# A hybrid decoder layer: 24 of 26 pairs of input-projection blocks in the seven-product form, the convolution one channel group at a time beside the heads, its norm late

## The chip, the core and the metric

The kernel runs on one core of a Trainium2 chip. Five engines work side by side, each through its own queue of instructions, in an order fixed when the program is built: TensorE (PE in the profile; its weight loads are PEld), VectorE (DVE), ScalarE (ACT), GpSimd (POOL) and SyncE (SP, which here only issues DMAs). They wait for each other through semaphores. The metric is device time in microseconds; a time without "median" is that of one profiled execution.

## The reference, cut to what matters

512 tokens of 2048 features are normalised and projected to 6664 features: three groups of 512 for a convolution branch, eight heads' queries, keys, values and gates (1024 each) with one forget logit per head, and queries and gates of a cross-attention (512 each). The three branches give 2048 features, projected back to 2048 and added to x; a final RMSNorm follows.

```python
h = rmsnorm(x, norm_g[l])
proj = h @ w_in[l]
u = cv_a * jax.nn.sigmoid(cv_b)
u = causal_depthwise_conv(u, conv_w[l], conv_b[l])          # 31 taps, per channel
u = jax.nn.silu(layernorm(u, conv_ln_g[l], conv_ln_b[l]))   # over the 512 channels
y_conv = (u @ w_conv_pw[l]) * jax.nn.silu(cv_gate)
logf = jax.nn.log_sigmoid(f_logit + b_f[l])                 # c = cumsum over the tokens
y_fox = fox_attention(fq, fk, fv, logf) * jax.nn.silu(fox_gate)
y_mem = memory_attention(mq, mk, mv) * jax.nn.silu(mem_gate)
x = x + jnp.concatenate([y_conv, y_fox, y_mem], -1) @ w_out[l]
```

Everything is float32. The kernel splits each operand of a large product into a high part (a cast to a shorter float32 form, by ScalarE) and a low part (the difference, by VectorE) and adds three matmuls: high x high, high x low, low x high.

## The kernel before

**Blocks.** Work goes by blocks of 128 output features. A weight block of 2048 x 128 arrives in two halves of [128, 8, 128] (`raw`, six buffers) and becomes `whi` and `wlo` (three buffers each). The normalised x, transposed, lies in sixteen 128-feature tiles as `hh` (high) and `hl` (low). `project` makes a plain block: 16 feature tiles x 3 matmuls (`mm3`, L104 to L106) over all 512 tokens.

**The seven-product form.** `pair` makes two blocks together. It cuts features and tokens into halves and forms seven products in place of eight, each of 8 feature tiles x 3 matmuls over 256 tokens (L729). For that it needs sums of quarters of h: `first_sums` makes s1, s2, s3 (tiles `s0`, `s1`, `s2` in the trace, each with a high part h and a low part l) through the temporary tiles `t`; `last_sum` makes a fourth, `s4`, and writes it over the quarter of h that holds features 0 to 1023 of tokens 256 to 511, after the last plain projection has read it. Per pair, VectorE makes seven `wlo`, four differences of weight blocks (`less`, L699) and two sums for the second block's output `col` (L696).

**The stages.** (1) Memory keys and values, x's norm (scaled on ScalarE, L212), its transposes. (2) Convolution inputs `C_A`, `C_B` for four channel groups, all plain, with the forget logits (`forget_logits`, `log_sigmoid`, `forget_columns`) between the first and the fourth. (3) Four memory queries and gates, plain, with their attention. (4) Four convolution gates, plain, with `first_sums` beside them, then the pointwise projection. (5) Eight heads: a pair for query and key, a pair for gate and value; the first of the sixteen pairs is plain (`PLAIN = 1`), and `last_sum` follows it. (6) The output projection, in steps.

**The convolution.** Each group's 31 taps are operations of 128x512 on one accumulator, the first on ScalarE (L323), thirty on VectorE (L328). They go to a list, `bg`, and `background(n)` takes n of them behind each projection of stages 2 and 3. Four accumulators stay in SBUF. `centre` and `normalise` make the norm over channels in the middle of stage 3's last head: a sum over the four groups, a matmul with `mean_r` for the mean over partitions, the same for the squares, Ln and Exp on ScalarE for the root, three VectorE steps, a multiplication of each group, then Silu and the split into `csh`/`csl`.

**The order.** Program order is not the order on the engines: a scheduler at build time orders each engine's instructions as they become ready in its own timeline. The pieces of order below are what it made of each version.

Of the kernel before, what the change touches and what calls it, by code (L numbers as in the profile page):

```python
# [10 lines left out]
F32 = mybir.dt.float32  # L11
# [6 lines left out]
P = 128  # L18
S = 512
# [15 lines left out]
PLAIN = 1  # L35
# [12 lines left out]
def hybrid_layer_kernel(  # L48
# [100 lines left out]
    cd = dr.tile([NH, S], F32, name="cd")  # L149

# [10 lines left out]
    mkv = mpool.enter_context(tc.tile_pool(name="mkv", bufs=1, side="right"))  # L161
# [5 lines left out]
    with tc.tile_pool(name="start", bufs=1) as st:  # L167
# [129 lines left out]
    def project(f0, per=0):  # L297
# [5 lines left out]
        background(per)  # L303
        return o

    def silu_of(pool, o, tag, bufs):

        sg = pool.tile([P, S], F32, tag=tag, name=nm(tag), bufs=bufs)
        nc.scalar.activation(sg, o, AF.Silu)
        return sg  # L310

# [3 lines left out]
    with tc.tile_pool(name="conv", bufs=1, reuse_waits="tile") as cp:  # L315
        cs = [tuple(cp.tile([P, S], F32R, name=f"cs{w}{c}") for w in "hl") for c in range(NC)]
        acc = [cp.tile([P, S], F32, tag=f"acc{c}", name=f"acc{c}") for c in range(NC)]

        def taps_of(c, up):
            a = acc[c]  # L320

            def first():
                nc.scalar.activation(  # L323
                    a, up[:, 0:S], AF.Identity, scale=cwt[:, c, 0:1], bias=conv_b_c(c)
                )

            def tap(j):
                return lambda: nc.vector.scalar_tensor_tensor(  # L328
                    a, up[:, j : j + S], cwt[:, c, j : j + 1], a, ALU.mult, ALU.add
                )  # L330

            bg.append(first)
            bg.extend(tap(j) for j in range(1, TAPS))

        def conv_in(c):
            oa = project(C_A + c * P, 6)
            ob = project(C_B + c * P, 6)
            up = cp.tile([P, PAD + S], F32, tag="up", name=nm("up"), bufs=3)
            nc.gpsimd.memset(up[:, 0:PAD], 0.0)
            sg = cp.tile([P, S], F32, tag="sgb", name=nm("sgb"), bufs=2)  # L340
            nc.scalar.activation(sg, ob, AF.Sigmoid)
            nc.vector.tensor_tensor(up[:, PAD:], oa, sg, ALU.mult)
            taps_of(c, up)

        def mem_query(ma, h):
            o = project(M_Q + h * P, 7)
            qh = ma.tile([P, S], F32R, tag="qh", name=nm("qh"), bufs=1)
            ql = ma.tile([P, S], F32R, tag="ql", name=nm("ql"), bufs=1)
            split(qh, ql, o)
            return qh, ql  # L350

        def mem_probs(ma, h, q):
            qh, ql = q
            pr = []
            for i2 in range(2):
                sp = at((P, 2, M))
                for j in range(2):
                    sl = slice((2 * i2 + j) * P, (2 * i2 + j + 1) * P)
                    mm3(sp[:, j, :], (qh[:, sl], ql[:, sl]), (mk[0][:, h, :], mk[1][:, h, :]), True, True)
                ng = ma.tile([P, 2], F32, tag="ng", name=nm("ng"), bufs=4)  # L360
                nc.vector.tensor_reduce(ng, sp, AX.X, ALU.max, negate=True)
                nc.vector.tensor_scalar(ng, ng, SC, None, ALU.mult)
                pp = ma.tile([P, 2, M], F32, tag="pp", name=nm("pp"), bufs=2)
                sm = ma.tile([P, 2], F32, tag="sm", name=nm("sm"), bufs=4)
                for j in range(2):
                    nc.scalar.activation(
                        pp[:, j, :], sp[:, j, :], AF.Exp,
                        bias=ng[:, j : j + 1], scale=SC, accum_out=sm[:, j : j + 1],
                    )
                nc.vector.reciprocal(sm, sm)  # L370
                for j in range(2):
                    nc.scalar.mul(pp[:, j, :], pp[:, j, :], sm[:, j : j + 1])
                pr.append(pp)
            return pr

        def mem_attend(ma, h, pr, gate):
            pts = []
            for mt in range(MT):
                tp = at()
                for i in range(NT):  # L380
                    nc.tensor.transpose(
                        tp[:, i * P : (i + 1) * P], pr[i // 2][:, i % 2, mt * P : (mt + 1) * P], ident
                    )
                th = ma.tile([P, S], F32R, tag="th", name=nm("th"), bufs=2)
                tl = ma.tile([P, S], F32R, tag="tl", name=nm("tl"), bufs=2)
                split(th, tl, tp)
                pts.append((th, tl))
            ov = at()
            for mt in range(MT):
                hs = slice(h * P, (h + 1) * P)  # L390
                mm3(ov, (mv[0][:, mt, hs], mv[1][:, mt, hs]), pts[mt], mt == 0, mt == MT - 1)
            nc.vector.tensor_tensor(gate, ov, gate, ALU.mult)
            nc.gpsimd.dma_start(out=yd[12 + h], in_=gate)

        fgs = {}

        def forget_logits(fg):
            wf = fg.tile([P, KT, NH], F32, name="wf")
# [3 lines left out]
            wfs = fg.tile([P, KT, P], F32R, name="wfs")  # L402
# [6 lines left out]
            f2 = fg.tile([2 * NH, S], F32, name="f2")  # L409
            nc.vector.tensor_copy(f2, fo[: 2 * NH, :])  # L410
            fl = fg.tile([NH, S], F32, name="fl")
            nc.gpsimd.dma_start(out=fl, in_=f2[NH : 2 * NH, :])
            fgs.update(f2=f2, fl=fl)

        def log_sigmoid(fg):
            z, e = fgs["f2"][:NH, :], fgs["fl"]
            nc.vector.tensor_tensor(z, z, e, ALU.add)
            nc.vector.tensor_scalar(z, z, bf_t, None, ALU.add)
            nc.vector.scalar_tensor_tensor(e, z, -1.0, z, ALU.mult, ALU.max)
            nc.scalar.activation(e, e, AF.Exp, scale=-1.0)  # L420
            u = fg.tile([NH, S], F32, name="u")
            nc.vector.tensor_scalar(u, e, 1.0, None, ALU.add)
            lu = fg.tile([NH, S], F32, name="lu")
            nc.scalar.activation(lu, u, AF.Ln)
            nc.vector.scalar_tensor_tensor(e, u, -1.0, e, ALU.add, ALU.subtract)
            nc.vector.reciprocal(u, u)
            nc.vector.tensor_tensor(e, e, u, ALU.mult)
            nc.vector.tensor_tensor(lu, lu, e, ALU.subtract)
            HALF = S // 2
            cs = [fg.tile([NH, HALF + S], F32, name=f"cs{i}") for i in range(2)]  # L430
            for t in cs:
                nc.vector.memset(t[:, :HALF], 0.0)
            nc.vector.scalar_tensor_tensor(cs[0][:, HALF:], z, 0.0, lu, ALU.min, ALU.subtract)
            cur, step = 0, 1

            def double(a, b, step):
                return lambda: nc.vector.tensor_tensor(
                    b[:, HALF:], a[:, HALF:], a[:, HALF - step : HALF - step + S], ALU.add
                )

            adds = []
            while step < S:
                adds.append(double(cs[cur], cs[1 - cur], step))
                cur, step = 1 - cur, 2 * step
            c = cs[cur][:, HALF:]
            adds.append(lambda: nc.gpsimd.dma_start(out=cd, in_=c))
            fgs["c"] = c
            for f in reversed(adds):
                bg.appendleft(f)

        def forget_columns():
            c = fgs["c"]
            pc = at((P, NT * NH))
            for i in range(NT):
                nc.tensor.transpose(
                    pc[:, i * NH : (i + 1) * NH], c[:, i * P : (i + 1) * P], ident[:NH, :NH]
                )
            nc.vector.tensor_scalar(ccol.rearrange("p i h -> p (i h)"), pc, -1.0, None, ALU.mult)
        conv_in(0)
        with tc.tile_pool(name="fg", bufs=1, reuse_waits="tile") as fg:  # L460
            forget_logits(fg)
            conv_in(1)
            log_sigmoid(fg)
            conv_in(2)
            forget_columns()
        conv_in(3)
        with tc.tile_pool(name="matt", bufs=1, reuse_waits="tile") as ma:

            gates = []
# [607 lines left out]
```

## Time and profile before

| what | value |
|---|---|
| median of 3 runs (lowest to highest) | 873.48 us (871.82 to 873.68) |
| the profiled execution | 872.15 us |
| its span, first to last instruction | 870.3 us |
| mean granted TensorE clock | 0.995 |
| TensorE matmuls | 5562 |
| taps on VectorE (L328) | 120, 747 ns the median |
| DMA | 107.52 MB, mean 124 GB/s |

A line of the timeline has start, duration, engine, line, operation, output and inputs with their shapes, and a count; an idle time before it stands in brackets. Durations of neighbours on one engine overlap a little, so the distance from one start to the next is what an operation costs in a full queue. A matmul's own duration (about 0.4 us for 512 columns) is longer than the distance to the next, since matmuls are pipelined. The activity by fortieths of the span (tenths busy):

```
PE   8999999999999999999999999999999999999996
DVE  4656699999956987877777777777777895876964
ACT  5894342225456643577565665657574852443523
```

Stage 2 and 3 are slices 4 to 12, the gates 13 to 15, the heads up to 31, the outputs the rest.

### The profile page before, as it was taken

How to read it: one execution, taken by the hardware profiler on the slowest of the kernel's cores; microseconds unless marked ns; L12 is line 12 of the kernel's file. 1: busy time of each engine (PE TensorE's matmuls, PEld its weight loads, DVE VectorE, ACT ScalarE, POOL GpSimd, SP SyncE). 2: the span in 40 equal slices, each digit the busy share in tenths (PEclk: the TensorE clock that was granted, in tenths of full speed). 3: DMA queues.
4: the chain of work that ended last, by engine and by line, in shares of the span. 5: the costliest groups of instructions: out<-in, count | busy, mean ns of one | idle time of the engine just before them, and what ended most of it. 6: DMA issues, size and time to landing. Idle time of an engine off the chain costs nothing.

```text
span 870.3 us, 13950 instructions
## 1 busy us (share of the span) xinstructions
PE 855.7 (98%) x5562; PEld 774.9 (89%) x5562; DVE 656.8 (75%) x948; ACT 463.8 (53%) x734; POOL 37.9 (4%) x76
## 2 busy tenths in 40 slices
PE   8999999999999999999999999999999999999996
PEld 6887887888888888999999999999999988998995
DVE  4656699999956987877777777777777895876964
ACT  5894342225456643577565665657574852443523
POOL 1001000000000002010001000000000000000001
PEclk9999999999999999999999999999999999999998
DMA  9972234333342334243434343333334745351415
GB/s 325 352 193 57 73 97 111 97 78 92 85 109 62 108 97 134 73 121 98 111 88 117 97 103 101 100 95 103 109 98 126 262 154 186 98 194 49 146 49 193
DMA packets 143265, 107.52 MB, mean 124 GB/s; under 512 B 3892, under 2 KB 126816, under 8 KB 142560
## 3 DMA queue, kind: packets, MB, share of 16 engines
q1 hardware_dynamic: 141696, 102.52, 40.4%
q0 software_dynamic: 1504, 4.11, 1.4%
q8 instruction: 43, 0.70, 0.3%
q14 instruction: 22, 0.18, 0.1%
HBM read 98.46 MB, written 8.14 MB: 122 GB/s over the span
## 4 chain that ended last, share of the span: by engine, by line
PE 96%; DVE 1%; issue 1%; DMA 1%; ACT 0%; SPq 0%; POOL 0%; POOLq 0%; ACTq 0%
PE pj L729 34%; PE pj L104 13%; PE pj L105 13%; PE pj L106 13%; PE pj L978 8%; PE at L104 3%; PE at L106 3%; PE at L105 3%; PE at L817 1%; DMA raw<-in_w_mem_kv_dram 1%; PE pj L262 0%; PE at L262 0%; PE pj L407 0%; PE pj L408 0%; PE at L778 0%
## 5 line engine op out<-in xcount | busy, mean ns | idle before, releaser
L93 ACT CAST whi<-raw 128x1024 fp32r<-128x1024 f32 x205 | 214.9, 1050 | 302.6 <-PE pj L105 115.1
L94 DVE TENSOR_TENSOR wlo<-raw,whi 128x1024 fp32r<-128x1024 f32 x205 | 250.2, 1222 | 121.2 <-ACT whi L93 116.7
L105 PE MATMUL pj<-hl,whi 128*128 128x512 f32 x352 | 139.6, 396 | 0.0
L106 PE MATMUL pj<-hh,wlo 128*128 128x512 f32 x352 | 139.4, 396 | 0.0
L104 PE MATMUL pj<-hh,whi 128*128 128x512 f32 x352 | 139.3, 396 | 0.0
L729 PE MATMUL pj<-hh,whi 128*128 128x256 f32 x480 | 135.4, 282 | 0.0
L729 PE MATMUL pj<-hl,whi 128*128 128x256 f32 x480 | 135.0, 281 | 0.0
L729 PE MATMUL pj<-hh,wlo 128*128 128x256 f32 x480 | 134.8, 281 | 0.0
L699 DVE TENSOR_TENSOR raw<-raw,raw 128x1024 f32<-128x1024 f32 x76 | 92.6, 1219 | 0.7
L729 PEld LDWEIGHTS pj<-hh,whi 128*128 128x128 f32 x480 | 90.5, 188 | 0.1
L729 PEld LDWEIGHTS pj<-hl,whi 128*128 128x128 f32 x480 | 90.5, 188 | 0.1
L729 PEld LDWEIGHTS pj<-hh,wlo 128*128 128x128 f32 x480 | 90.5, 188 | 0.0
L328 DVE SCALAR_TENSOR_TENSOR acc<-up,cwt,acc 128x512 f32<-128x512 f32 x120 | 84.5, 744 | 1.2 <-ACT acc L323 0.9
L978 PE MATMUL pj<-whi,rh 128*128 128x256 f32 x448 | 79.9, 279 | 0.7 <-DVE sst L1032 0.4
L104 PEld LDWEIGHTS pj<-hh,whi 128*128 128x128 f32 x352 | 66.1, 188 | 15.9 <-DVE hl L97 0.2
L106 PEld LDWEIGHTS pj<-hh,wlo 128*128 128x128 f32 x352 | 66.1, 188 | 15.7
L105 PEld LDWEIGHTS pj<-hl,whi 128*128 128x128 f32 x352 | 66.2, 188 | 15.5
L978 PEld LDWEIGHTS pj<-whi,rh 128*128 128x128 f32 x448 | 68.8, 188 | 1.3 <-DVE res L904 1.1
L978 PE MATMUL pj<-wlo,rh 128*128 128x256 f32 x224 | 62.3, 279 | 0.0
L978 PEld LDWEIGHTS pj<-wlo,rh 128*128 128x128 f32 x224 | 42.1, 188 | 0.2
L729 PE MATMUL pj<-s0l,whi 128*128 128x256 f32 x120 | 34.4, 286 | 0.0
L729 PE MATMUL pj<-s0h,whi 128*128 128x256 f32 x120 | 34.3, 286 | 0.0
(295 smaller groups left out, 1676.7 us busy)
## 6 DMA issues: line engine op xcount, KB each, us to landing
raw<-in_w_in_dram SPq DMA_DIRECT2D x104, 512.0 KB, 3.8
raw<-in_w_out_dram SPq DMA_DIRECT2D x32, 512.0 KB, 4.6
raw<-in_w_mem_kv_dram SPq DMA_DIRECT2D x12, 512.0 KB, 7.3
xr<-in_x_dram SPq DMA_DIRECT2D x4, 1024.0 KB, 7.9
res<-in_x_dram SPq DMA_DIRECT2D x8, 512.0 KB, 7.2
out_dram<-res SPq DMA_DIRECT2D x16, 256.0 KB, 2.7
rs<-yd SPq DMA_DIRECT2D x15, 256.0 KB, 4.9
mr<-in_mem_dram SPq DMA_DIRECT2D x8, 256.0 KB, 7.3
```

Of the source, the lines that this page charges most:

```text
L93: ins = nc.scalar.copy(hi, src)
L94: nc.vector.tensor_tensor(lo, src, hi.bitcast(F32), ALU.subtract)
L104: nc.tensor.matmul(o, ah, bh, start=start, stop=False)
L105: nc.tensor.matmul(o, ah, bl, start=False, stop=False)
L106: nc.tensor.matmul(o, al, bh, start=False, stop=stop)
L328: return lambda: nc.vector.scalar_tensor_tensor(a, up[:, j : j + S], cwt[:, c, j : j + 1], a, ALU.mult, ALU.add)
L699: nc.vector.tensor_tensor(o, p, q, ALU.subtract)
L729: nc.tensor.matmul(o, p[:, k, :], q, start=start and k == 0 and i == 0, stop=k == HK - 1 and i == 2, skip_group_check=True,)
L817: nc.tensor.transpose(tp[:, (i - j) * P : (i - j + 1) * P], pr[i][:, j * P : (j + 1) * P], ident)
L978: nc.tensor.matmul(o[:, m, :], p, q[:, k, :], start=start and k + m + i == 0, stop=k == HK - 1 and i == 2, skip_group_check=True,)
```

## The change

- `PLAIN` and `plain_pair` are gone. Plain are only group 0's convolution inputs and memory head 0's query and gate. Memory heads 1 to 3, all head pairs, convolution groups 1 to 3 and the four convolution gates (two pairs) use `pair`: 24 of 26.
- `first_sums` and `last_sum` run at once, around memory head 0's two projections, with doubled temporary tiles; the log-sigmoid and its running sum (nine doublings, `cs`) follow in the program.
- The convolution pairs stand behind heads 0, 2 and 4. Each group has one `up` and one `acc`; its taps go to `bg`, of which each of a pair's seven products takes one; then the accumulator is stored to DRAM (`accd`) through GpSimd's queue.
- Behind head 6, the head tiles are given up for a norm pool, the four accumulators are read back, and the two gate pairs follow. `centre` and `normalise` come behind the first gate pair (squares now on ScalarE), the pointwise projection behind the second, then the head tiles again for head 7.
- x's row scaling moves from ScalarE to VectorE; the memory keys and values move to the other side of SBUF.

```diff
-            nc.scalar.mul(xrows[t], xrows[t], rs)
+            nc.vector.tensor_scalar(xrows[t], xrows[t], rs, None, ALU.mult)
...
+    with tc.tile_pool(name="fg", bufs=1, reuse_waits="tile") as fg:
+        oa, ob = project(C_A), project(C_B)
+        conv_channels(0, [oa], ob)
+        forget_logits(fg)
+        with tc.tile_pool(name="stmp", bufs=2, reuse_waits="tile") as stmp:
...
+            for g in range(4):
+                first_sums(tmp, g)
+            oq, og = project(M_Q), project(M_G)
+            for g in range(4):
+                last_sum(tmp, g)
+        forget_columns(log_sigmoid(fg))
...
+            background(1)
...
+    def conv_channels(c, xs, gate):
+
+        background(len(bg))
+        up = cp.tile([P, PAD + S], F32, tag="up", name=nm("up"))
+        acc = cp.tile([P, S], F32, tag="acc", name=nm("acc"))
...
+        bg.append(first)
+        bg.extend(tap(j) for j in range(1, TAPS))
+        bg.append(lambda: nc.gpsimd.dma_start(out=accd[c], in_=acc))
...
+    def open_norm():
+        lp = ln["pool"] = lnpool.enter_context(tc.tile_pool(name="ln", bufs=1, reuse_waits="tile"))
+        background(len(bg))
+        acc = ln["acc"] = [lp.tile([P, S], F32, name=f"la{c}") for c in range(NC)]
+        for c in range(NC):
+            nc.gpsimd.dma_start(out=acc[c], in_=accd[c])
...
+    def after_gates(i):
+        def f(xs, col):
...
+            if i == 0:
+                centre()
+                normalise()
+            else:
+                project_conv()
+                lnpool.close()
+                open_fox()
...
+    work = [(M_Q + h * P, M_G + h * P, after_mem(h)) for h in range(1, NM)]
+    for h in range(NH):
+        work.append((F_Q + h * P, F_K + h * P, after_qk(h)))
+        work.append((F_G + h * P, F_V + h * P, after_gv(h)))
+        if h in (0, 2, 4):
+            c = h // 2 + 1
+            work.append((C_A + c * P, C_B + c * P, after_conv(c)))
+        if h == NH - 2:
+            for i in range(2):
+                g = C_G + 2 * i * P
+                work.append((g, g + P, after_gates(i)))
```

In the new kernel the split's low part is L93, `mm3` is L103 to L105, the seven products are L493, the weight differences L463, the taps L367.

**First place: VectorE behind the weights of memory head 0.** Before, VectorE goes from the third weight half (`wlo_1119`) to group 0's `up`, four taps, the copy of the forget logits (`f`, L410) and more taps:

```order
L94 TENSOR_TENSOR wlo_1119<-raw_1116,whi_1118 128x1024
L342 TENSOR_TENSOR up_998<-pj_888,sgb_1000 128x512
L328 SCALAR_TENSOR_TENSOR acc_872<-up_998,cwt,acc_872 128x512 x4
L410 COPY f_1045<-pj_1012 16x512
L328 SCALAR_TENSOR_TENSOR acc_872<-up_998,cwt,acc_872 128x512 x3
L417 TENSOR_TENSOR f_1045<-f_1045,fl 8x512
L328 SCALAR_TENSOR_TENSOR acc_872<-up_998,cwt,acc_872 128x512
```

Now the sums of h (`t`, L311, from `hh` and `hl`) stand behind that copy (L392), and a tap follows six of them:

```order
L93 TENSOR_TENSOR wlo_1199<-raw_1196,whi_1198 128x1024
L359 TENSOR_TENSOR up_1020<-pj_910,up_1020 128x512
L367 SCALAR_TENSOR_TENSOR acc_1021<-up_1020,cwt,acc_1021 128x512 x4
L392 COPY f_1025<-pj_1036 16x512
L311 TENSOR_TENSOR t_119_1075<-hh_105,hl_106 128x512
L311 TENSOR_TENSOR t_120_1076<-hh_113,hl_114 128x512
L311 TENSOR_TENSOR t_121_1077<-hh_105,hl_106 128x512
L311 TENSOR_TENSOR t_122_1090<-hh_107,hl_108 128x512
L311 TENSOR_TENSOR t_123_1091<-hh_115,hl_116 128x512
L311 TENSOR_TENSOR t_124_1092<-hh_107,hl_108 128x512
L367 SCALAR_TENSOR_TENSOR acc_1021<-up_1020,cwt,acc_1021 128x512
```

The sums have come from the gate stage to the time of memory head 0's projections, among the same taps and the same forget chain as before.

**Second place: the end of the sums, on VectorE and on TensorE.** The last operations of `last_sum` (`t`, L329; `hl`, L93) alternate with taps and with the doublings of `cs` (L417):

```order
L329 TENSOR_TENSOR t_151_1278<-t_151_1278,t_152_1279 128x512
L417 TENSOR_TENSOR cs_1287<-cs_1286 8x512
L367 SCALAR_TENSOR_TENSOR acc_1021<-up_1020,cwt,acc_1021 128x512
L93 TENSOR_TENSOR hl_110<-t_149_1271,hh_109 128x2x256
L417 TENSOR_TENSOR cs_1286<-cs_1287 8x512
L93 TENSOR_TENSOR hl_112<-t_151_1278,hh_111 128x2x256
L367 SCALAR_TENSOR_TENSOR acc_1021<-up_1020,cwt,acc_1021 128x512
L417 TENSOR_TENSOR cs_1287<-cs_1286 8x512
L367 SCALAR_TENSOR_TENSOR acc_1021<-up_1020,cwt,acc_1021 128x512 x6
L431 TENSOR_SCALAR ccol<-at_1311 128x32
```

TensorE, in the first pair (memory head 1, product with `s4`, output `pj_1373`), reads these `hl` and has the four transposes of `cs` (L428) among them:

```order
L493 MATMUL pj_1373<-hl_110,whi_1498 128x256
L493 MATMUL pj_1373<-hh_109,wlo_1499 128x256
L493 MATMUL pj_1373<-hh_111,whi_1498 128x256
L493 MATMUL pj_1373<-hl_112,whi_1498 128x256
L493 MATMUL pj_1373<-hh_111,wlo_1499 128x256
L428 MATMUL at_1311<-ident,cs_1287 128x8 x4
L493 MATMUL pj_1373<-hh_111,whi_1498 128x256
L493 MATMUL pj_1373<-hl_112,whi_1498 128x256
L493 MATMUL pj_1373<-hh_111,wlo_1499 128x256
L493 MATMUL pj_1374<-s2h_884,whi_1528 128x256
```

Before, those transposes (L455) stood inside a plain projection of convolution group 2, which reads nothing of the sums; now they stand where TensorE also reads the last of the sums.

**Third place: TensorE at the norm's second mean matmul** (L484 before, L607 now; `csl` is the low part of the summed squares). Before, plain matmuls of the memory gate follow, and the pointwise projection starts 184 rows later:

```order
L104 MATMUL pj_2383<-hh_105,whi_2373 128x512
L105 MATMUL pj_2383<-hl_106,whi_2373 128x512
L106 MATMUL pj_2383<-hh_105,wlo_2374 128x512
L484 MATMUL pj_2310<-csl_865,mean_r 128x512
L104 MATMUL pj_2383<-hh_107,whi_2373 128x512
L105 MATMUL pj_2383<-hl_108,whi_2373 128x512
L106 MATMUL pj_2383<-hh_107,wlo_2374 128x512
```

Now the first matmuls of the pointwise projection (`csh_7547`, the normalised group 0) follow at once, and a product of the next pair (`pj_7469`) comes behind them:

```order
L493 MATMUL pj_7203<-hl_120,whi_7499 128x256
L493 MATMUL pj_7203<-hh_119,wlo_7500 128x256
L607 MATMUL at_7293<-csl_7290,mean_r 128x512
L103 MATMUL pj_7530<-csh_7547,whi_7536 128x512
L103 MATMUL at_7531<-csh_7547,whi_7536 128x512
L103 MATMUL pj_7532<-csh_7547,whi_7536 128x512
L103 MATMUL at_7533<-csh_7547,whi_7536 128x512
L493 MATMUL pj_7469<-s0h_868,whi_7638 128x256
L493 MATMUL pj_7469<-s0l_869,whi_7638 128x256
```

The projection has moved up against the mean whose result it needs.

More of the change, by code (lines that the diff above doesn't have):

```diff
@@ L34 @@
 WARM = 16
-PLAIN = 1
 C_A, C_B, C_G = 0, CW, 2 * CW
@@ L302, in project @@
             mm3(o, w(k), (h_hi[k], h_lo[k]), k == 0, k == KT - 1)
-        background(per)
         return o
[L306 to L310, printed above, removed]
     NC = CW // P
     PAD = TAPS - 1
[L315 to L398, printed above, removed]
@@ new lines, in hybrid_layer_kernel, with plus, less @@
+    ppool = ctx.enter_context(ExitStack())
+    pp_ = ppool.enter_context(tc.tile_pool(name="pair", bufs=1, side="right", reuse_waits="tile"))
+    a11 = [quarter(g, 0, 0) for g in range(4)]
+    a12 = [quarter(g, 1, 0) for g in range(4)]
+    a22 = [quarter(g, 1, 1) for g in range(4)]
+    s4 = [quarter(g, 0, 1) for g in range(4)]
+    s1, s2, s3 = sums
+    def plus(o, p, q):
+        nc.vector.tensor_tensor(o, p, q, ALU.add)
+    def less(o, p, q):
+        nc.vector.tensor_tensor(o, p, q, ALU.subtract)
@@ new lines, in gate_values @@
+    def gate_values(xs, col):
+        fx = fox["pool"]
+        gate = fx.tile([P, S], F32, tag="fgate", name=nm("fgate"), bufs=2)
+        for x_, g in zip(xs, halves(gate)):
+            nc.scalar.activation(g, x_, AF.Silu)
+        vp = at()
+        for j in range(NT):
+            sl = slice(j * P, (j + 1) * P)
+            nc.tensor.transpose(vp[:, sl], col[:, sl], ident)
+        v = tuple(fx.tile([P, NT, P], F32R, tag=t, name=nm(t)) for t in ("vh", "vl"))
+        split(*v, vp.rearrange("p (j d) -> p j d", d=P))
+        return gate, v
```

678 lines of the change are left out of this document (354 added, 324 removed).

## The prediction

> **What bounds the kernel now.** I read the page's busy table and chain first, then TensorE's own waits, then busy time by stage. The columns of the first line are busy us, share of the span, instructions.
>
> ```profile
> PE 855.7 (98%) x5562; PEld 774.9 (89%) x5562; DVE 656.8 (75%) x948; ACT 463.8 (53%) x734; POOL 37.9 (4%) x76
> ...
> PE 96%; DVE 1%; issue 1%; DMA 1%; ACT 0%; SPq 0%; POOL 0%; POOLq 0%; ACTq 0%
> ```
>
> TensorE is busy for 98% of the span and is 96% of the chain that ended last. Its waits (waiting line, releaser, us, times, longest) are few, and both of the large ones lie in the opening stage:
>
> ```profile
> PE pj L104 <- ACT mh L96: 2.5, 1, 2.5
> PE pj L262 <- DVE kt L284: 1.8, 1, 1.8
> ```
>
> By stage (us; then busy us of PE, PEld, DVE, ACT, POOL; clock; DMA share), the convolution's inputs, the gates and one whole head:
>
> ```profile
> 77.50:147.00 69.50, 69.50 (x299) 55.76 (x299) 54.22 (x73) 22.42 (x24) 3.86 (x6) 1.00 0.35 89
> 283.40:330.00 46.60, 46.60 (x202) 37.77 (x202) 41.86 (x60) 23.63 (x34) 1.61 (x3) 1.00 0.40 112
> 449.70:494.86 45.16, 45.16 (x376) 44.89 (x376) 33.83 (x48) 28.30 (x49) 2.18 (x5) 1.00 0.39 106
> ```
>
> From 77.5 us until the outputs TensorE never pauses, so each microsecond of matmul taken away is a microsecond gained, but only while VectorE (DVE), already at 33.83 of 45.16 us in a head, keeps up. The change takes from the first and adds to the second.
>
> **What it removes.** Start-to-start times, first a plain matmul (36 steps from the first row to the last, all of one form), then 120 matmuls of a seven-product pair:
>
> ```profile
> 83.84 0.40 PE L104 MATMUL pj<-hh,whi 128*128 128x512 f32 x1
> ...
> 92.24 0.40 PE L104 MATMUL pj<-hh,whi 128*128 128x512 f32 x1
> ```
> ```profile
> 521.00 14.20 PE pj L729 x120
> ```
>
> That is 8.40/36 = 0.2333 us for 512 columns and 14.20/120 = 0.1183 us for 256. A plain pair is 2x16x3 = 96 of the first, 22.4 us; a seven-product pair is 7x8x3 = 168 of the second, 19.9 us. Nine more pairs change form (24 for 15): 9 x 2.53 = **-22.7 us**. Attention, transposes, pointwise projection and outputs keep their matmuls. Weight bytes are the same.
>
> **What VectorE must now do at once.** The seven-product form needs the sums s0, s1, s2 and the reused quarter (the low parts `hl` written last). Before, they were spread over the gate stage (count, shortest/median/longest ns, first and last start):
>
> ```profile
> L556 DVE TENSOR_TENSOR t<-hh,hl x16: 629/685/694, 293.9 to 353.8; 128x512 f32<-128x512 f32 x16
> ...
> L94 DVE TENSOR_TENSOR hl<-t,hh x4: 682/684/686, 342.9 to 360.2; 128x512 fp32r<-128x512 f32 x4
> ```
>
> Now the second memory pair wants them right after two plain projections. The order shows where VectorE starts on them: behind the copy of the forget logits, which waits for TensorE's forget matmuls. Before has that copy too, with a time, and prices around it:
>
> ```profile
> 100.60 0.68 DVE L410 COPY f<-pj 16x512 f32<-16x512 f32 x1
> ...
> 104.69 0.47 DVE L418 TENSOR_SCALAR f<-f,bf_t 8x512 f32<-8x512 f32 x1
> 105.09 0.73 DVE L328 SCALAR_TENSOR_TENSOR acc<-up,cwt,acc 128x512 f32<-128x512 f32 x1
> 105.75 0.67 DVE L419 SCALAR_TENSOR_TENSOR fl<-f 8x512 f32<-8x512 f32 x1
> 106.35 0.73 DVE L328 SCALAR_TENSOR_TENSOR acc<-up,cwt,acc 128x512 f32<-128x512 f32 x1
> 107.10 1.23 DVE L94 TENSOR_TENSOR wlo<-raw,whi 128x1024 fp32r<-128x1024 f32 x1
> 108.24 0.75 DVE L328 SCALAR_TENSOR_TENSOR acc<-up,cwt,acc 128x512 f32<-128x512 f32 x1
> ...
> 111.31 3.33 DVE L426 RECIPROCAL u<-u 8x512 f32<-8x512 f32 x1
> 114.57 0.64 DVE L328 SCALAR_TENSOR_TENSOR acc<-up,cwt,acc 128x512 f32<-128x512 f32 x1
> ```
> ```profile
> 300.11 0.69 DVE L94 TENSOR_TENSOR s2l<-t,s2h 128x512 fp32r<-128x512 f32 x1
> 300.71 0.68 DVE L567 TENSOR_TENSOR t<-t,t 128x512 f32<-128x512 f32 x1
> 301.32 0.68 DVE L556 TENSOR_TENSOR t<-hh,hl 128x512 f32<-128x512 f32 x1
> ```
> ```profile
> L94 DVE TENSOR_TENSOR wlo<-raw,whi 128x1024 fp32r<-128x1024 f32 x205 | 250.2, 1222 | 121.2 <-ACT whi L93 116.7
> ...
> L699 DVE TENSOR_TENSOR raw<-raw,raw 128x1024 f32<-128x1024 f32 x76 | 92.6, 1219 | 0.7
> ```
>
> I price by start-to-start, since neighbours overlap: a sum or a low part of 512 takes 0.605, a tap 0.66, a step of 8x512 0.60, a weight's low part 1.14, the weight difference (same mean) also 1.14, the reciprocal 3.26. From the copy to the ninth doubling of `cs`, on which TensorE's `L428` transposes wait, the order has 52 sums and low parts (31.5), 8 weight low parts (9.1), 6 differences (6.8), 18 taps of group 0 (11.9) and the forget chain with its copy (13.7): **73.0 us**, so from 100.6 to 173.6. In that time TensorE has 96 plain matmuls (22.4) and 117 of the first pair (13.8): it stands at the transposes at 136.8 and waits **36.8 us**. The last `hl` is only 1.3 us earlier, so moving the transposes would save almost nothing. Next in order are six more taps at once (0.74 each, chained), `ccol`, half of `col` and `ql`, so `ql` at 179.1; TensorE would want it at 141.1. I take **+38.0**. Ends: 31 if neighbouring operations overlap better, 45 if each chained one pays another 0.1.
>
> Behind it VectorE recovers: a memory pair has no taps left and some 17 us of VectorE (7 low parts, 4 differences, two sums of 256: 13.2; query, probabilities and gate about 4) beside 23.5 us of TensorE.
>
> **The norm, late.** Before, 184 rows of TensorE's order stood between the second mean matmul and the pointwise projection; now none. TensorE waits through the whole chain. Its parts, from before's own norm:
>
> ```profile
> 277.61 1.28 ACT L505 ACT_TABLE_LOAD   x1
> 278.91 0.63 ACT L505 ACTIVATE up<-up 128x512 f32<-128x512 f32 x1
> ...
> 280.49 1.28 ACT L506 ACT_TABLE_LOAD   x1
> 281.79 0.64 ACT L506 ACTIVATE up<-up 128x512 f32<-128x512 f32 x1
> ...
> 286.84 1.53 ACT L514 ACTIVATE acc<-acc,cols 128x512 f32<-128x512 f32 x2
> 288.26 0.61 ACT L93 CAST csh<-acc 128x512 fp32r<-128x512 f32 x1
> ```
> ```profile
> 282.46 0.69 DVE L507 TENSOR_TENSOR up<-up,up 128x512 f32<-128x512 f32 x1 [0.72 <-ACT up L506]
> ...
> 284.63 2.50 DVE L511 TENSOR_TENSOR acc<-acc,up 128x512 f32<-128x512 f32 x4
> ```
>
> ScalarE (ACT) first has the cast of `whi_7638` and a gate (about 1.2), then load and Ln 1.9, load and Exp 1.9; VectorE three steps 2.17 and the first product 0.6; ScalarE two Silu (0.71 each; their load hides beside VectorE) and the cast 0.61: **+9.8**. Ends: 0, if the matmuls of the pair that is ready stood ahead, and 14, if the accumulators, read back behind head 6's store, hold VectorE. That store's row gives a landing of 2.4 us for 256 KB; four loads at that pace have the 15 us of matmuls that TensorE still holds as cover:
>
> ```profile
> yd<-fgate POOLq DMA_DIRECT2D x7, 256.0 KB, 2.4
> ```
>
> The Trainium skill, "ScalarE: Activation LUTs", section Table sets, says that Ln followed by Exp needs one table load, as one set holds both. The rows show a load of 1.28 us for each, and the new order lists both; by the page the term would be 8.5.
>
> **The clock after a wait.** Before shows it once, after the opening wait for weights (PEclk is the last column but two):
>
> ```profile
> 6.00:8.00 2.00, 0.53 (x5) 0.29 (x3) 0.00 (x0) 0.44 (x1) 0.00 (x0) 1.00 1.03 373
> 8.00:10.00 2.00, 0.96 (x2) 0.58 (x3) 1.36 (x2) 2.00 (x5) 0.00 (x0) 0.63 1.06 400
> 10.00:12.00 2.00, 2.00 (x7) 1.61 (x7) 2.00 (x4) 1.04 (x3) 0.00 (x0) 0.51 1.05 409
> 12.00:14.00 2.00, 2.00 (x10) 1.57 (x10) 1.55 (x3) 1.02 (x2) 0.00 (x0) 1.00 1.05 385
> ```
>
> Granted 0.63 and 0.51 for 4 us, then 1.00: 0.74 + 0.98 = 1.7 us lost for one long wait. I charge 1.7 behind the norm and 1.0 behind the sums, where the `ql` wait hides the rest: **+2.7**; ends 0 and 6. [...]
>
> **What is hidden.** Row scaling moves from ScalarE to VectorE (4 of 128x2048, not in the trace: between 1.6 by the 0.40 of `L418` and 2.4 by four sums). It lies where TensorE waited 1.8 us for `kt`; I take **-1.0**, ends -1.8 and +2. Nine pairs add 27 casts and 27 copies to ScalarE, which is busy 53%. Four stores of an accumulator go through GpSimd's queue behind its mask selects; the next group starts a whole pair later. In the heads, five pairs (two heads and one convolution pair) now cost VectorE 2 x 33.83 + 13.2 + 30 taps (19.8) + 0.7 = 101.4 us beside TensorE's 5 x 19.9 + 2 x 5.4 = 110.2: 92%. I take 0; if that cover goes, TensorE waits up to 3 us in each of seven heads.
>
> **Sum**, against the profiled execution: 870.3 - 22.7 - 1.0 + 38.0 + 9.8 + 2.7 = 897.1 span; outside the span it had 1.85 us (872.15), so **899 us**. The median of the three runs before, 873.48, lies 1.3 above that execution, well inside the range.
>
> **Rivals.**
> - *The norm is covered*, because the pair's ready matmuls fill the gap: 899 less 9.8 and its 1.7 of clock, 887. The order, with the projection's first matmul right behind the mean, speaks against it. 0.13.
> - *VectorE starves the heads too.* At 92% a burst (a head's probabilities with taps and weight parts) may outrun the three weight buffers: 1 to 3 us in seven heads, some 914. VectorE was 75% busy before and TensorE never waited on it. 0.15.
> - *Faster.* The place is the first pair after the two plain projections. If VectorE gets through the sums sooner, by starting them before 100.6, or by leaving taps and forget chain until later, the wait shrinks. It decides at 27 us less: a wait under 11 and the change wins; with none, 872.15 - 22.7 - 1.0 + 9.8 + 1.7 = 860. Against it: the queue's order has the sums behind that copy with taps between them. 0.07.
> - *The form gains nothing*, 256-column matmuls running slower than 0.1183 beside the denser VectorE: 899 + 22.7 = 922. Fifteen pairs show the rate steady. 0.03.
> - A balance of these within 0.2% of before: 0.02.
>
> Forecast 0.60, between 892 and 906. The range takes in the covered norm, most of the starved heads and the ends of the sums term: **884 to 915**, leaving out the faster cases, the 922 and the tails. About 0.2% is what a measurement of this kernel can tell from no change. Faster 0.08, same 0.02, slower 0.90.
>
> **What would show it.** TensorE's waits after: on VectorE's `s0l`, `s1l`, `hl`, `cs` and `ql`, about 38 us together, between 126 and 180 us, VectorE near 100% busy there; one wait of 8 to 11 us on ScalarE's `csh` near the end of the projections; seven-product matmuls still 0.118 us apart; a clock near 0.5 in the sums stretch. I am wrong if VectorE shows idle time in that stretch, if the wait there is under 25 us, or if heads show waits over 1 us on `wlo`.

## The result and the profile after

The changed kernel takes **902.40 us** (median of 4 runs, 901.92 to 902.68), the kernel before 873.30 (871.82 to 873.68): 1.0336 times as long, 95% interval 1.0318 to 1.0354. The profiled execution has a span of 900.0 us, 29.7 more than before; forecast were 897.1 of span and 899 of time.

The page: busy us, share and instructions of each engine, the activity by fortieths of the span (22.5 us each) with the granted clock, and the shares of the chain that ended last.

```profile
PE 845.5 (94%) x6210; PEld 800.3 (89%) x6210; DVE 729.6 (81%) x1037; ACT 504.4 (56%) x799; POOL 55.1 (6%) x84
PE   8999964599999999999999999999959999999996
DVE  4684899987777889979899798997957895886864
PEclk9999986699999999999999999999979999999999
...
PE 87%; DVE 8%; issue 2%; ACT 2%; DMA 1%; SPq 0%; POOL 0%; POOLq 0%; ACTq 0%; DVEq 0%
```

TensorE was 96% of the chain before and VectorE 1%; now 87% are TensorE's and 8% VectorE's. Two dents stand in TensorE's row: slices 6 to 8 (112 to 180 us), with VectorE at 9 and the clock at 0.6 to 0.8 beside them, and slice 30, near 660 us. TensorE's waits (us in total, times, longest) name the same two places, where before had 2.5 and 1.8 us in the opening:

```profile
PE pj L493 <- ACT p L467: 16.6, 2, 16.4
PE pj L103 <- ACT csh L92: 10.0, 1, 10.0
PE pj L493 <- DVE s1l L93: 6.7, 2, 3.8
PE pj L493 <- ACT s0h L92: 3.6, 1, 3.6
```

**The sums.** VectorE's timeline, its copy of the forget logits and the last doubling of `cs`:

```profile
98.10 0.68 DVE L392 COPY f<-pj 16x512 f32<-16x512 f32 x1
...
170.19 0.67 DVE L417 TENSOR_TENSOR cs<-cs 8x512 f32<-8x512 f32 x1
```

From 98.10 to 170.8 are 72.7 us of one unbroken queue; forecast were 73.0. TensorE's timeline, the first matmul of memory head 0 and the transposes of `cs`:

```profile
97.90 0.40 PE L103 MATMUL pj<-hh,whi 128*128 128x512 f32 x1
...
172.29 0.59 PE L428 MATMUL at<-ident,cs 8*128 8x8 f32 x4
```

74.4 us lie between them, for 22.4 + 13.8 = 36.2 us of matmuls: **38.2 us lost**. The largest wait is put down to the copy `p`; ScalarE's timeline shows what held that copy:

```profile
165.30 0.62 ACT L92 CAST hh<-t 128x512 fp32r<-128x512 f32 x1 [9.00 <-DVE t L329]
166.56 0.62 ACT L92 CAST hh<-t 128x512 fp32r<-128x512 f32 x1 [0.65 <-DVE t L329]
167.09 0.37 ACT L467 COPY p<-pj 128x256 f32<-128x256 f32 x1
```

The copy is one of a queue in order: it stands behind the last casts of `last_sum`, and these wait for VectorE. So the name in the row is ScalarE's, and the cause is VectorE's queue. By stage (us; then busy us of PE, PEld, DVE, ACT, POOL; clock; DMA share), that wait, and the matmuls behind it:

```profile
147.00:167.40 20.40, 1.43 (x5) 1.14 (x5) 20.40 (x31) 3.74 (x7) 0.00 (x0) 0.50 0.20 51
167.50:172.20 4.70, 4.69 (x21) 4.55 (x21) 4.66 (x8) 2.60 (x4) 0.51 (x1) 0.50 0.00 0
```

21 matmuls of 256 columns took 4.7 us there for 2.5, at a granted clock of 0.50.

**The norm.** The second mean on TensorE, the first matmul of the projection, and ScalarE's table loads between:

```profile
656.85 0.39 PE L607 MATMUL at<-csl,mean_r 128*128 128x512 f32 x1
667.22 0.80 PE L103 MATMUL pj<-csh,whi 128*128 128x512 f32 x1 [9.98 <-ACT csh L92]
```
```profile
658.34 1.28 ACT L639 ACT_TABLE_LOAD   x1
...
660.28 1.28 ACT L640 ACT_TABLE_LOAD   x1
...
662.22 1.28 ACT L668 ACT_TABLE_LOAD   x1
```

**The heads.** Five pairs (two heads and a convolution pair) in one window:

```profile
372.98:484.26 111.28, 110.96 (x916) 109.76 (x915) 99.57 (x140) 69.70 (x111) 8.14 (x12) 1.00 0.39 107
```

VectorE is busy for 89% of it and TensorE waits for almost nothing.

### The profile page after: what moved, and what is told of

It reads as the page before. It is cut to its first block, busy times and chain, and to the rows that moved or that the text cites. A ratio compares the mean times of both kernels' runs of the same rounds, so it can differ in the third digit from the quotient of the medians.

```text
span 900.0 us, 15460 instructions
## 1 busy us (share of the span) xinstructions
PE 845.5 (94%) x6210; PEld 800.3 (89%) x6210; DVE 729.6 (81%) x1037; ACT 504.4 (56%) x799; POOL 55.1 (6%) x84
## 4 chain that ended last, share of the span: by engine, by line
PE 87%; DVE 8%; issue 2%; ACT 2%; DMA 1%; SPq 0%; POOL 0%; POOLq 0%; ACTq 0%; DVEq 0%
PE pj L493 51%; PE pj L1004 8%; PE pj L103 5%; PE pj L104 5%; PE pj L105 5%; PE at L103 3%; PE at L105 3%; PE at L104 3%; DVE wlo L93 1%; DVE raw L463 1%; DVE acc L367 1%; PE at L839 1%; DVE t L311 1%; DMA raw<-in_w_mem_kv_dram 1%; PE pj L391 0%
## 5 line engine op out<-in xcount | busy, mean ns | idle before, releaser
L93 DVE TENSOR_TENSOR wlo<-raw,whi 128x1024 fp32r<-128x1024 f32 x232 | 283.0, 1222 | 90.5 <-ACT whi L92 88.9
L493 PE MATMUL pj<-hh,whi 128*128 128x256 f32 x768 | 218.5, 284 | 17.0 <-ACT p L467 16.6
L493 PE MATMUL pj<-hl,whi 128*128 128x256 f32 x768 | 217.3, 283 | 0.0
L493 PE MATMUL pj<-hh,wlo 128*128 128x256 f32 x768 | 216.1, 283 | 0.0
L493 PEld LDWEIGHTS pj<-hh,whi 128*128 128x128 f32 x768 | 146.0, 190 | 18.7 <-ACT p L467 17.7
L493 PEld LDWEIGHTS pj<-hl,whi 128*128 128x128 f32 x768 | 146.0, 190 | 0.5
L493 PEld LDWEIGHTS pj<-hh,wlo 128*128 128x128 f32 x768 | 145.6, 190 | 0.1
L463 DVE TENSOR_TENSOR raw<-raw,raw 128x1024 f32<-128x1024 f32 x112 | 136.6, 1219 | 0.8
L367 DVE SCALAR_TENSOR_TENSOR acc<-up,cwt,acc 128x512 f32<-128x512 f32 x120 | 89.6, 746 | 1.3 <-ACT acc L362 0.9
L493 PE MATMUL pj<-s1l,whi 128*128 128x256 f32 x192 | 55.1, 287 | 6.7 <-DVE s1l L93 6.7
L493 PE MATMUL pj<-s0h,whi 128*128 128x256 f32 x192 | 56.3, 293 | 3.6 <-ACT s0h L92 3.6
L493 PE MATMUL pj<-s1h,whi 128*128 128x256 f32 x192 | 55.3, 288 | 1.7 <-ACT whi L92 1.7
L493 PE MATMUL pj<-s0h,wlo 128*128 128x256 f32 x192 | 55.5, 289 | 1.3 <-DVE wlo L93 1.3
L493 PE MATMUL pj<-s1h,wlo 128*128 128x256 f32 x192 | 55.6, 290 | 0.6 <-DVE wlo L93 0.5
L493 PE MATMUL pj<-s0l,whi 128*128 128x256 f32 x192 | 54.9, 286 | 0.2 <-DVE s0l L93 0.2
L493 PE MATMUL pj<-s2l,whi 128*128 128x256 f32 x192 | 54.0, 281 | 0.0
L493 PE MATMUL pj<-s2h,wlo 128*128 128x256 f32 x192 | 54.0, 281 | 0.0
L493 PE MATMUL pj<-s2h,whi 128*128 128x256 f32 x192 | 53.9, 281 | 0.0
```

The lines of the kernel that those rows point to most:

```text
L93: nc.vector.tensor_tensor(lo, src, hi.bitcast(F32), ALU.subtract)
L367: return lambda: nc.vector.scalar_tensor_tensor(acc, up[:, j : j + S], cwt[:, c, j : j + 1], acc, ALU.mult, ALU.add)
L463: nc.vector.tensor_tensor(o, p, q, ALU.subtract)
L493: nc.tensor.matmul(o, p[:, k, :], q, start=start and k == 0 and i == 0, stop=k == HK - 1 and i == 2, skip_group_check=True,)
```

## The experiments

Below, **time lost** in a stretch is the sum, over TensorE's rows, of the distance to the next start less the matmul's own (0.2333 us for 512 columns, 0.1183 for 256). In the changed kernel it is 38.9 in the sums stretch (117 to 180 us), 2.0 beside the rest of the memory heads and head 0 (180 to 280), 7.8 in the heads, 11.9 around the norm (640 to 690).

**Taps away from the sums** (`taps_held`). The first tap's bias is made to depend on the last `hl`:

```diff
+            hl3 = quarter(3, 0, 1)[1][:, 1, M - 1 : M].bitcast(F32)
+            nc.vector.scalar_tensor_tensor(held, hl3, 0.0, conv_b_c(0), ALU.mult, ALU.add)
...
-                acc, up[:, 0:S], AF.Identity, scale=cwt[:, c, 0:1], bias=conv_b_c(c)
+                acc, up[:, 0:S], AF.Identity, scale=cwt[:, c, 0:1], bias=held if c == 0 else conv_b_c(c)
```

> The first tap's bias is made to depend on the last low part of the sums, so that no tap of group 0 runs before the sums are done: 18 taps of 0.66 us and the 4 before them leave the stretch, and run beside the memory pairs later, where VectorE has room. Theory (each microsecond of VectorE's work in the stretch is one of TensorE's wait): 18 x 0.66 = 11.9 us less, 890.5 us, 888 to 893. Rival (taps sit in gaps that the sums leave while they wait for ScalarE's casts): no gain, above 899. Second rival (the taps are paid again beside the memory pairs): between 895 and 902.

Measured 890.90 us, 11.5 less. The last doubling of `cs` starts at 159.47, for 170.19, and the copy of the forget logits, with no taps ahead of it, waits for TensorE:

```profile
99.29 0.68 DVE L393 COPY f<-pj 16x512 f32<-16x512 f32 x1 [4.02 <-PE pj L392]
...
159.47 0.67 DVE L418 TENSOR_TENSOR cs<-cs 8x512 f32<-8x512 f32 x1
```

From the copy to the last doubling VectorE's queue takes 60.8 us for 72.7: the 11.9 that were priced. TensorE's gain is another sum: the lost time in the stretch falls by 9.2, to 29.7, about 4 come back beside the memory pairs (the second rival, in part), and the heads lose about 5 less, for a reason that no run isolates. That the total comes so near to 11.9 is partly luck.

**Sums first** (`sums_first`, `sums_room`). `first_sums` moves ahead of `project(C_A)`; in the second kernel the forget weights get a place of their own:

```diff
+        with tc.tile_pool(name="stmp", bufs=2, reuse_waits="tile") as stmp:
+            for g in range(4):
+                first_sums(tmp, g)
         oa, ob = project(C_A), project(C_B)
         conv_channels(0, [oa], ob)
         forget_logits(fg)
```

> The sums s0, s1, s2 of h are formed ahead of the first convolution input instead of behind it; the amount of VectorE's work is the same. Theory (the loss in the sums stretch is VectorE's amount of work between its free start and TensorE's need): VectorE stood idle for 13.0 us between 77.6 and 98.1, and can use all of it, so TensorE's loss of 38.9 falls to about 26: 902.4 - 13 = 889.4 us, 887 to 893. Rival (the loss is the ping-pong between VectorE and ScalarE's casts at the end, with last_sum): little moves, above 898.

Measured 900.71: nearly nothing, and by neither theory. TensorE's largest wait is a new one:

```profile
PE pj L390 <- DVE wfs L93: 19.5, 1, 19.5
```

The pool of the forget weights took the space that the temporaries held, so these weights came only after the sums (`wfs` at 110.63), and TensorE stood at the forget matmuls before any of memory head 0's. The stretch had become cheap and the wait had moved ahead of it. With room for both:

> As sums_first, but the forget weights' tiles (cut from 128 to 64 padded columns) stand beside the sums' temporaries, which are single now, so that no tile waits for another's space. Theory (VectorE's amount of work from its free start on): the 19.5 us wait on wfs is gone, the 13.0 us of idle time before 98.1 are used, and the loss in the sums stretch falls from 38.9 to about 26: 902.4 - 13 = 889.4 us, 887 to 894. Rival (the single temporaries make each sum wait for ScalarE's cast, or the loss sits in last_sum): above 897.

Measured **889.13**, 13.3 less; the lost time is 24.3 for 38.9. The last doubling of `cs` starts 11.2 us earlier, and TensorE is at the transposes 12.6 us earlier:

```profile
159.70 0.41 PE L427 MATMUL at<-ident,cs 8*128 8x8 f32 x4 [0.73 <-DVE cs L416]
```

So 12 us of work taken out of VectorE's queue, and 13 us of idle time given to it, each bring about that much: the sums term is a matter of how much work stands in VectorE's queue behind its free start, not of ScalarE's casts.

**The norm** (`norm_early`, `proj_late`, `warm_norm`). First the norm's place in the program alone:

```diff
-            if i == 0:
-                centre()
-                normalise()
-            else:
+            if i == 1:
...
                 fpool.close()
                 open_norm()
+                centre()
+                normalise()
```

> The norm's two means, root and scaling stand ahead of the first gate pair instead of behind it; nothing else moves. Theory (the norm term is a chain that TensorE waits through because nothing stands between it and the projection): with 40 us of gate matmuls in between, the wait of 10.0 us on csh and the 1.8 us of slow matmuls behind it go: 902.4 - 11.8 = 890.6 us, 889 to 893. Rival (the chain's VectorE and ScalarE work only displaces weight parts of the gate pairs, and TensorE waits on those instead): above 896.

Measured 902.56, the wait unchanged:

```profile
PE pj L103 <- ACT csh L92: 10.0, 1, 10.0
```

The edit moved nothing on the engines. VectorE's first addition of the norm stands at the same row and starts at 631.38 us, for 631.07; the scheduler had already put it behind the landing of the accumulators, whose loads are issued from 623 on behind head 6's store. The place in the program was not what set its time, and my theory of this run overlooked that. The other end can be moved:

```diff
-            else:
-                project_conv()
-                lnpool.close()
-                open_fox()
...
+            if h == NH - 1:
+                project_conv()
+                lnpool.close()
+                open_fox()
             pr.update({h: probs(h, *queries_keys(xs, col))})
```

> The pointwise projection stands behind head 7's query and key pair instead of ahead of it; means, root and scaling stay. The order has 129 of TensorE's rows (15 us) between the second mean and the projection now, for 0 in the changed kernel. Theory (the norm's chain ends when it ends, and the term is only what TensorE lacks to do meanwhile): the wait on csh of 10.0 us and the 1.8 us of slow matmuls go: 902.4 - 11.8 = 890.6 us, 889 to 893. Rival (the projection's four accumulation banks or head 7's tiles, free only later now, hold the next pair): above 896.

Measured 894.48, 7.9 less. 15 us of matmuls stand in the gap now, and 2.2 us of wait are left, since the chain itself takes longer, with a pair's weight parts among its steps on VectorE and ScalarE: from the second mean to the first `csh` 17.7 us (659.64 to 677.36), for 10.3 (656.85 to 667.17). Behind that wait the clock is at 0.50 for 3.4 us (677.99 to 681.41), so the time lost around the norm is 3.8 for 11.9.

```profile
PE pj L103 <- ACT csh L92: 2.2, 1, 2.2
```

The third run leaves the chain as it is and gives TensorE something to do:

```diff
+        ln["low"] = lo
...
+        warm = at()
+        for i in range(36):
+            nc.tensor.matmul(warm, mean_r, ln["low"], start=True, stop=True)
```

> 36 matmuls of 128x512 whose result nobody reads are added behind the norm's second mean, ready when that mean is: 36 x 0.2333 = 8.4 us of filler inside the 10.0 us wait on csh. Theory (behind a long wait TensorE is granted half its clock, which costs 1.8 us beside the wait): the granted clock stays at 1.00 around the projection, the wait shrinks to under 2 us, and the time falls by 1.5 to 2.0 us, to 900.4 to 900.9. Rival (the slow matmuls behind the wait are the new operands' or the profile's doing, not the idle time's): 902.4, the clock still near 0.5 behind the filler. Against both: fillers that delay the projection, above 903.

Measured 900.14, 2.3 less, with *more* matmuls. The windows of the changed kernel behind its wait, then of this one at the same place:

```profile
665.00:667.00 2.00, 0.00 (x0) 0.00 (x0) 1.91 (x4) 1.86 (x3) 0.00 (x0) 0.50 0.00 0
667.00:669.00 2.00, 1.78 (x4) 1.50 (x5) 1.26 (x2) 2.00 (x4) 0.00 (x0) 0.50 0.00 0
669.00:671.00 2.00, 2.00 (x10) 1.91 (x10) 0.12 (x1) 0.39 (x2) 0.00 (x0) 0.50 0.00 0
671.00:673.00 2.00, 2.00 (x14) 1.83 (x13) 0.00 (x0) 0.00 (x0) 0.00 (x0) 0.90 0.00 0
```
```profile
653.00:670.00 17.00, 15.42 (x89) 13.16 (x89) 11.94 (x15) 11.74 (x15) 0.00 (x0) 1.00 0.33 91
```

The clock is 1.00 throughout with the filler, whose wait on `csh` is 1.6 us, and 0.50 for 4 us behind the wait without it: the clock term is a cost of its own beside the wait.

**The form** (`plain_four`). Four head pairs made by `project` twice:

```diff
+    def plain_pair(fa, fb):
+        oa, ob = project(fa), project(fb)
...
+        background(7)
...
-            steps = pair(fa, fb)
+            steps = (plain_pair if F_G + P <= fa <= F_G + 4 * P else pair)(fa, fb)
```

> The changed kernel with the gate and value pairs of heads 1 to 4 in the plain form; since the quarter of h that the sums overwrote is read there as it is, these four pairs compute something else than the reference. Theory (a pair in the plain form costs TensorE 22.4 us, in the seven-product form 19.9, whatever VectorE does): 4 x 2.53 = 10.1 us more, 912.5 us, 911 to 914. Rival (beside a VectorE that is 90% busy the seven-product form already loses its gain to waits on differences and weight parts): 902 to 907.

Measured 911.62, 9.2 more (9.9 by the spans, 909.9 and 900.0): 2.3 to 2.5 us for a pair. The seven-product form earns what the rate of its matmuls says.

**Plain memory heads** (`plain_mem`).

```diff
-            for g in range(4):
-                last_sum(tmp, g)
...
+            steps = (plain_pair if n < NM - 1 else pair)(fa, fb)
             next(steps)
+            if n == NM - 2:
+                for g in range(4):
+                    last_sum(lambda tag: pp_.tile([P, 2, M], F32, tag="col", name=nm("t"), bufs=2), g)
```

> Memory heads 1 to 3 use plain pairs again, and last_sum comes behind them; all else is the changed kernel's. Theory: three pairs at 2.53 us cost 7.6 us of matmuls, and the sums have three pairs more of cover, so the loss of 38.9 us falls to 0 to 4: 902.4 + 7.6 - 38.9 + 2 = 873 us, 871 to 876. Rival (what TensorE waits for is not the sums but taps and forget chain, whatever the form): above 885. Second rival (the seven-product form gains nothing beside a full VectorE): under 868.

Measured 889.75: a miss by 17. The number lies in the first rival's range, but not by its mechanism: TensorE reaches the transposes of `cs` at 164.94 without a wait. (One thing more differs: these plain pairs take no taps from `bg`; group 0's last tap still runs at 170.7, for 178.2.) The wait in the old place is gone (1.5 us lost up to 167), and 19.3 us are lost from there to 280:

```profile
98.00:200.00 102.00, 100.84 (x474) 82.49 (x473) 84.97 (x121) 41.48 (x65) 2.30 (x5) 1.00 0.28 76
200.00:262.00 62.00, 53.53 (x387) 50.35 (x387) 48.63 (x73) 40.27 (x76) 3.41 (x6) 0.92 0.29 82
```

VectorE is not full in either window, so the amount of its work alone does not explain this loss: TensorE's rows there show waits of 1 to 3 us on memory heads' `ql` and `tl` and on head 0's `fk`, with the clock down to 0.92. Why VectorE serves these late, with `last_sum` among them, I did not take apart; it stays open.

**x's scaling** (`x_act`), line L212 as before.

> x's row scaling goes back from VectorE to ScalarE, all else as changed. Theory of the prediction (the move to VectorE gains 1.0 us): 903.4. Theory from the trace (the changed kernel's opening stage lost 13.3 us beside its matmuls, for 16.5 before, and the missing wait on kt is 1.8 of these): 904.2 to 905.6, the wait on kt back. Rival (the opening differs for another reason, the memory tiles' other side): 902.4.

Measured 905.93, 3.5 more; the wait on `kt` is back, and the forget copy starts at 101.21, for 98.10:

```profile
PE pj L262 <- DVE kt L284: 1.9, 1, 1.9
```

From 60 to 70 us, where that wait and the transposes of x behind it lie, the lost time is 5.4 us before, 2.1 in the changed kernel and 5.4 again here. The move from ScalarE to VectorE is the whole of the opening's gain, and it is larger than forecast.

**Together** (`combo`, `far`, `thirds`). `sums_room` and `proj_late`, with taps and forget chain both held until the last `hl`:

> All 24 pairs stay in the seven-product form; sums first with their own room, taps of group 0 and the forget chain held until the last low part of the sums, projection behind head 7's first pair. Theory: VectorE's 73.0 us from the copy to the last step lose 13.0 (earlier start), 11.9 (taps) and 11.8 (forget chain without its copy and first addition), 36.3 remain, and TensorE has 36.2 us of matmuls there: the loss of 38.9 falls to 0 to 4; the norm's 11.8 go too: 902.4 - 37 - 11.8 = 853.6 us, 851 to 858, under the kernel before. Rival (work that is held is paid beside the memory pairs, where VectorE has 23.5 us per pair and 17 us of its own): 860 to 872.

Measured 875.17, 1.0021 times the kernel before (1.0011 to 1.0030): 21.6 us over the theory, and over the rival too. TensorE no longer waits for a sum; but the transposes of `cs` stand in the first pair, and what was held is now ahead of them:

```profile
PE at L428 <- DVE cs L417: 22.8, 1, 22.8
```

So the forget chain goes back to where it can run early, and only the taps are held, until memory head 1's gate:

> Sums first with their own room, projection behind head 7's first pair, as in combo; but the forget chain runs as early as it can, and group 0's taps are held until memory head 1's gate is there, so that they come beside memory heads 2 and 3 and head 0. Theory (only what VectorE has to do between its free start and TensorE's need counts): 73.0 - 13.0 - 11.9 = 48.1 us from 98.1, so the last running sum at 146.2, where TensorE stood at the transposes at 142.9 in combo: the wait of 22.8 us there falls to about 3, and with it most of the 5 us of slow matmuls behind it: 875.2 - 27.9 + 4 = 851.3 us, 849 to 856, under the kernel before. Rival (the taps are paid again beside the memory pairs and head 0): 857 to 868.

Measured **867.63**, 0.9944 times the kernel before (0.9931 to 0.9957). The last doubling ends at 147.7 us, 146.2 was forecast, and the wait at the transposes is 1.0 us. But 12.4 us are lost between 180 and 280 (1.1 in `combo`), and the time is 16.3 over the theory: the rival, taps paid again, held. They ran in one row, so in the last run they are held in three parts:

```diff
+        coef = lambda j: held[:, j // 10 : j // 10 + 1] if c == 0 and j in (10, 20) else cwt[:, c, j : j + 1]
...
+                was = (conv_b_c(0), cwt[:, 0, 10:11], cwt[:, 0, 20:21])[h - 1]
+                nc.vector.scalar_tensor_tensor(held[:, h - 1 : h], gate[:, 0:1], 0.0, was, ALU.mult, ALU.add)
```

> As far, but group 0's taps are held in three parts: ten wait for memory head 1's gate, ten for head 2's, ten for head 3's. In far 11 us more than in combo were lost between 180 and 280 us, on weight parts and on head 0's query and key, beside taps that came as fast as VectorE took them. Theory (VectorE's load there is under TensorE's time on the whole, and only its bunching costs): with ten taps, 6.6 us, for each pair of 23.5 us with 17 us of VectorE's own work, most of that goes: 867.6 - 7 = 860.6 us, 858 to 864. Rival (the load there is too much however it is spread, or it moves on to head 0): 866 to 870.

Measured **862.59**, 0.9878 times the kernel before (0.9861 to 0.9894). The same window of `far`, then of this kernel:

```profile
180.00:262.00 82.00, 74.07 (x587) 71.91 (x586) 68.23 (x99) 52.63 (x93) 4.85 (x9) 0.96 0.37 100
```
```profile
180.00:262.00 82.00, 78.54 (x646) 76.14 (x645) 71.80 (x108) 55.52 (x103) 4.61 (x10) 1.00 0.38 101
```

With more work on VectorE in the same 82 us, TensorE does more, and the clock stays at 1.00. Between 180 and 280 about 5 us are still lost, so bunching was most of the cost, not all. This version, with the seven-product form of the change, is 10.6 us under the kernel before and 39.8 under the changed one.

## Why the prediction was right, point by point

- **Matmuls, -22.7.** Held: `plain_four` gives 2.3 to 2.5 us for a pair, 2.53 was taken.
- **Opening, -1.0.** Right sign, too small: the forget copy is 2.5 us earlier (98.10 for 100.60), and `x_act` loses 3.5. I had counted the wait on `kt` and set a price on VectorE against it; the transposes of x behind that wait also came faster (3.3 us less lost from 60 to 70).
- **Sums, +38.0.** 38.2 up to the transposes. VectorE's queue was priced right (72.7 us for 73.0), and the runs that took 11.9 out of it and started it 13.0 earlier gained 11.5 and 13.3. That 38.0 and 38.2 lie so close is partly luck: 38.0 was the wait for `ql`, with 36.8 at the transposes, and the difference came from slow matmuls instead. The step that failed is the name of the last wait: not `ql`, which was in time, nor `cs`, but the last `hh`, by way of the copy behind it. Nothing in the sum hangs on it, because the matmuls behind that wait ran at half the clock, and VectorE kept ahead of them.
- **Clock, +1.0 in the sums, +1.7 at the norm.** Together about right: the waits of the stretch are 29.9 us and the rest of the 38.2 is mostly slow matmuls, which lie under VectorE's 72.7 us except for those behind the last wait. Behind the norm it is 1.9 (11.9 lost, 10.0 of it wait).
- **Norm, +9.8.** 10.0, with the table loads for Ln and for Exp that the order had shown. The Trainium skill, "ScalarE: Activation LUTs", section Table sets, expects one load for the two; the rows have two of 1.28 us, and a third for Silu.
- **Heads, 0.** Nearly: five pairs take 111.3 us, 110.2 was the sum; that is about 1 us for five pairs, by estimate 3 to 4 in all, and no wait on `wlo` over 0.3. This, and the opening, are the two terms that were off; they have opposite signs and partly cancel. What makes a pair dearer no run takes apart.
- **Sum.** -22.7 - 2.5 + 38.2 + 11.9 + 3.5 = 28.4 of the 29.7 us.

Of the rivals, the covered norm fell by the order, as was argued. The faster one named its own condition, sums begun before 100.6 or taps left until later; `thirds` does both and is faster, with the projection moved as well.

## What to carry to other kernels

A form that saves time on the bounding engine can move its preparation, all at once, ahead of its first use on another engine: add up that engine's queue from its free start to the instruction that the bounding engine needs, and compare it with the work that the bounding engine has until then. Work that is due later (here the taps) can be held back by a real dependency, and then spread; an edit of the program's order alone may move nothing (`norm_early`), or only move the wait (`sums_first`). A tile that has to share space with others can be such a wait.

## What the hardware showed that was not expected

The granted clock falls for short waits as well. In the changed kernel TensorE waited 1.34 us until 124.88 and 3.62 us until 129.94:

```profile
123.00:126.00 3.00, 1.66 (x14) 1.46 (x13) 3.00 (x5) 0.36 (x1) 0.00 (x0) 1.00 0.00 0
126.00:129.00 3.00, 0.32 (x3) 0.12 (x1) 3.00 (x2) 0.00 (x0) 0.00 (x0) 0.95 0.00 0
129.00:132.00 3.00, 0.58 (x1) 0.29 (x1) 3.00 (x5) 1.51 (x2) 0.00 (x0) 0.50 0.00 0
```

The first left it at 1.00. In the second the fall came before the wait was over: a mean of 0.95 from 126 to 129 is 0.3 us at half, so TensorE had been idle for 2.4 us. In `far` a wait of 2.23 us (207.36 to 209.59) was enough:

```profile
206.89:210.30 3.41, 0.97 (x7) 0.57 (x5) 1.16 (x2) 3.40 (x4) 0.00 (x0) 1.00 0.00 0
210.30:213.71 3.41, 3.17 (x15) 3.17 (x16) 3.41 (x5) 3.39 (x6) 0.00 (x0) 0.50 0.00 0
213.72:217.13 3.41, 3.41 (x31) 3.41 (x31) 3.39 (x5) 3.04 (x9) 0.00 (x0) 1.00 0.44 108
```

The Trainium skill, "TensorE: Matmul & The Clock Gate", section HAM oscillation, gives the rule as no idle gaps over about 3.4 us. These rows do not agree with it as a limit on a single wait, and neither does the kernel before, whose clock fell at a wait of 2.5 us in the opening.

In the traces the clock changes in steps of 3.41 us: in the changed kernel it fell at 128.69, rose at 138.93, fell at 145.76 and rose at 173.07, which are 3, 2 and 8 steps. Counted by such steps in all fourteen profiles, each step at full clock in which TensorE was idle for 1.85 us or more is followed by one at 0.50, and none with 1.40 or less is; between them both occur (1.47 in `sums_first` brought 0.50, 1.83 in `thirds` did not). This is read from the traces; no run was made to test it.

Behind the waits of 10.0 and 16.4 us the half clock lasted 4.2 and 5.6 us, and 36 matmuls that nobody reads, laid into the 10.0 us wait, took 2.3 us off the time.
